# A hybrid decoder layer on one core: the first gate spread by POOL's queue one slab earlier, x's rows loaded slab by slab, the last modulation's bias from diagonal blocks

## The chip, the cores and the metric

The kernel runs on one core of a Trainium2 chip. The metric is the device time of one execution in microseconds; of several executions the median is given. Beside it stands one execution that the hardware profiler recorded, with a trace of every instruction.

## What is computed

One layer (DEPTH = 1) of a conditioned decoder trunk on x of 256 rows and 2048 columns, all in float32. The parts that matter here, cut from the reference:

```
mod = (c_act @ ada_w[l] + ada_b[l])[:, None, :]
sh1, sc1, g1, sh2, sc2, g2 = jnp.split(mod, N_MOD, axis=-1)
h = modulate(rms_norm(x, norm1_g[l]), sh1, sc1)
proj = h @ w_in[l] + b_in[l]
...
merged = gate_lru * (y_lru @ w_lru_out[l]) + gate_attn * (y_attn @ w_attn_out[l])
x = x + g1 * (merged @ w_o[l])
h2 = modulate(rms_norm(x, norm2_g[l]), sh2, sc2)
gate, up = jnp.split(h2 @ w_ffn_in[l], 2, axis=-1)
x = x + g2 * ((jax.nn.silu(gate) * up) @ w_ffn_out[l])
...
return rms_norm(x, final_g)
```

The six modulation vectors come from one vector c through a 2048 x 12288 matrix. g1 is the first gate, g2 the last modulation; final_g is the gain of the last norm.

## The kernel before, in words

**Items.** All large products are a list of items, made by `add_slab` and its relatives in the order in which they run: w_in, the gates of the recurrent branch, w_lru, the gates of the attention branch, w_att, w_o, the first and the second FFN matrix. An item is one weight load `raw` of 128 partitions x 1024 float32 (512 KB). Each weight is split into a high part `hi` (ACT, L305) and the rest `lo` (DVE, L317), and each product is three matmuls (hi with hi, hi with lo, lo with hi), L355 to L357. An item of w_att or w_o has twelve matmuls of 512 columns: two 128-row pieces of the weight, two halves of the 256 rows, three products. Eight items make a slab of 512 output columns; `wa` and `wo` are the sums in PSUM. In a slab's last item the matmuls of the first half of the rows stand first.

**Order.** Nothing is reordered by a scheduler: each engine and each queue runs in the order in which `step` writes the program. Per item, `step` issues the load six items ahead (L288), makes `hi` four ahead and `lo` three ahead, calls what is hung onto the item (`before`), writes the matmuls, and lets "sides" put in their own work while a clock of estimates says that there is room (`run_sides`, with an allowance `clock["slack"]`). What follows a slab is a generator in `posts`, one step of it per item. All loads and stores are DMAs on SP's queue; a DMA there waits until its buffer is free, and those behind it wait with it. Rows of POOL are few.

**Buffers.** `raw` has five buffers, `hi` four, `lo` three; everything of 4 KB per partition that lives longer (`b4`) shares 25.

**The modulation.** Five of the six vectors are sums over the columns of a transposed matrix: 158 loads `aw` of 512 KB, one DVE pass each (L496), with the row `crow` as the second operand; `modc[:, m, kt]` gets the results, the first gate (m = 2) ahead of the two parts of the second norm. The last one, g2, is needed as a row: `ada_rows` adds 32 loads `aw` of ada_g, scaled by c, into `pa` (L685, one DVE pass each, two per 128 rows), and a product with a matrix of ones (L691) sums the partitions. `pa` uses the buffer of `crow` and is set up like this:

```
        pa = ap_.tile([P, D], F32, tag="pal", name="pa")
        nc.gpsimd.memset(pa, 0.0)
        nc.sync.dma_start(pa[0:1, :], bg_row)
```

**The first gate and w_o.** g1 lies in 16 columns of `modc`. `gate_rows` transposes them on PE (L1011), copies the 16 x 128 result (ACT, L1013), writes it to DRAM as `g1d` (L1015) and reads it back twice, spread over all partitions (L1018). `load_rows` loads x's rows, four tiles `xr` of 512 columns (L1034). Both are hung onto the fourth item of w_o's first slab (`late` 6 means the weight's rows from 6 x 128 on). After each of the first three slabs `o_post` multiplies by the gate (L1055), adds x (L1057), takes squares and stores the rows as `x1d` (L1041).

**The second norm.** `second_norm` follows w_o's last slab: product with the gate and x's row (L1100, L1101), squares, root, transposes on PE (L1080), and the scaled, shifted rows for the first FFN slab `fg`. `ada_ffn`, the side that runs `ada_rows`, goes on before and after it.

**The last stage.** The second FFN matrix is done in two halves of the columns. Rounds of items alternate: two plain ones and four in which seven products stand for eight (L355 to L357 into `pp`, `pq`, `pr`, `pu`), whose third and fourth weights `made` are differences taken on DVE (L418 to L425, tile `last`). When the first half's last item is done, the post of `blocks(0, 2)` adds four blocks to x (L1415, L1417) and then multiplies by the final gain (L1441), once per half of the rows.

Of the kernel before, what the change touches and what calls it, by code (L numbers as in the profile page):

```python
# [11 lines left out]
AF = mybir.ActivationFunctionType  # L12
# [4 lines left out]
P = 128  # L17
D = 2048
S = 256
NK = D // P  # L20
# [13 lines left out]
V_ADA = V_CB + 64  # L34
# [23 lines left out]
SLACK = (2.0, 2.0)  # L58
# [14 lines left out]

@with_exitstack
def hybrid_layer(
    ctx: ExitStack, tc, vecs, x_t, x_r, ada_k, ada_t, ada_g, w_in, bv_row, bm_row, bg_row, lru_w, w_lru, w_att, w_o,
    w_f1, w_f2a, w_f2d, w_f2b, w_f2c, fg_row, out,
):
    nc = tc.nc
# [44 lines left out]
    vec = const.tile([P, NV], F32, name="vec")  # L124
# [18 lines left out]
    ident = const.tile([P, P], F32, name="ident")  # L143
# [134 lines left out]
    items = []  # L278
# [389 lines left out]
    def ada_rows():  # L668

        got = Halves([ada_g[kt, :, j * CH:(j + 1) * CH] for kt in range(NK) for j in range(2)])  # L670
        got.spare = lambda: len(got.got) - got.own < N_SPARE
        yield 0, 0, 0, 0, lambda: ada.cost is None
        streams.append(got)
        got.fetch()

        pa = ap_.tile([P, D], F32, tag="pal", name="pa")
        nc.gpsimd.memset(pa, 0.0)
        nc.sync.dma_start(pa[0:1, :], bg_row)
        for kt in range(NK):
            for j in range(2):  # L680
                if not got.got:
                    got.fetch()
                yield CH * T_DVE, 0, 0, 0, got.here
                p = pa[:, j * CH:(j + 1) * CH]
                nc.vector.scalar_tensor_tensor(p, got.take(), cact[:, kt:kt + 1], p, op0=ALU.mult, op1=ALU.add)  # L685
                got.fetch()
        for c in range(4):
            yield 0, 0, 0, 1
            pb = mtile(f"pb{c}")
            cs = slice(c * 512, (c + 1) * 512)  # L690
            nc.tensor.matmul(pb, lhsT=ones, rhs=pa[:, cs], start=True, stop=True)  # L691
            yield 0, 0.55
            nc.scalar.copy(pa[:, cs], pb)
            free(m=1)
        bcs[5] = pa
# [311 lines left out]
    def gate_rows():  # L1007
        while not {(2, kt) for kt in range(NK)} <= cols_done:
            ada.advance(True)
        ps = mtile("g1_ps")  # L1010
        nc.tensor.transpose(ps[0:NK, 0:P], modc[:, 2, :], ident)  # L1011
        row = sp.tile([P, S], F32, tag="t2", name="g1_row")
        nc.scalar.copy(row[0:NK, 0:P], ps[0:NK, 0:P])  # L1013
        free(m=1)
        nc.sync.dma_start(g1d, row[0:NK, 0:P])  # L1015
        for i in range(2):
            g1.append(b4(f"g1{i}", F32, (CH,)))
            nc.sync.dma_start(  # L1018
                g1[i], g1d[8 * i:8 * i + 8, :].rearrange("k p -> (k p)").partition_broadcast(P)
            )  # L1020

    for s in range(4):
        add_slab(w_att[s], f"wa{s}", aact, 0, NK, att_post(s), True)


    x1d = dp.tile([S, D], F32, name="x1d")
# [1 line left out]
    xr, x1T, pts = [], {}, {}  # L1028
    ss2 = const.tile([P, 2, 4], F32, name="ss2")

    def load_rows():
        for s in range(4):
            xr.append(b4(f"xr{s}", F32, (2, 512)))
            nc.sync.dma_start(xr[s], x_r[:, s * 512:(s + 1) * 512].rearrange("(t p) n -> p t n", p=P))  # L1034

    def w_o_first():
        load_rows()
        gate_rows()

    def keep_rows(s):  # L1040
        nc.sync.dma_start(x1d[:, s * 512:(s + 1) * 512].rearrange("(t p) n -> p t n", p=P), xr[s])  # L1041
# [23 lines left out]

    mact = of(m_hi, m_lo)

    def x_first():
        ada.finish(halves.fetch)

    for s in range(4):
        add_slab(w_o[s], f"wo{s}", mact, 0, NK, o_post(s), True, (w_o_first, None, None, x_first)[s], 6 if s == 0 else 0)

    def turn(p, of_w=False):

# [14 lines left out]

    def second_norm(banks):
        sides[:] = [ada_ffn]
        both = h2["both"] = hp.tile([P, NK, 2, S], F32R, tag="h", name="h2_both")
        hh, hl = both[:, :, 0, :], both[:, :, 1, :]

# [330 lines left out]
    def blocks(n0, n1):  # L1426

        def post():
            last = None
            for n in range(n0, n1):  # L1430
                for t in range(2):
                    g = residual(t, n)
                    next(g)
                    if last is not None:
                        next(last, None)
                    last = g
                    yield 1.2, 0.7
            next(last, None)
            for t in range(2):
                x2 = fin["x2"][:, t, n0 * 512:n1 * 512]  # L1440
                nc.vector.tensor_tensor(x2, x2, fin["fg"][:, n0 * 512:n1 * 512], op=ALU.mult)  # L1441
                yield 0.6 * (n1 - n0), 0.7 * (1 - t)
        return post
# [191 lines left out]
def _layout(i):  # L1635
# [6 lines left out]
    def slabs(w):  # L1642
        n = w.shape[1] // 512
        return w.reshape(NK, P, n, 512).transpose(2, 1, 0, 3).reshape(n, P, NK * 512)

    def pairs(w):
# [15 lines left out]
    made = {  # L1662
        "vecs": vecs, "x_t": f("x")[0].T.reshape(NK, P, S).transpose(1, 0, 2), "x_r": f("x")[0], "ada_k": a_k,
        "ada_t": a_t, "ada_g": ada_w[:, 5 * D:].reshape(NK, P, D),
        "w_in": slabs(f("w_in")[0]), "bv_row": f("b_in")[0, 6656:7168], "bm_row": f("b_in")[0, 7168:], "bg_row": ada_b[None, 5 * D:], "lru_w": lru,
        "w_lru": slabs(f("w_lru_out")[0]), "w_att": slabs(f("w_attn_out")[0]), "w_o": slabs(f("w_o")[0]),
        "w_f1": slabs(f("w_ffn_in")[0]), "w_f2a": w2[:, :CH].reshape(NH, P, CH),
        "w_f2d": w2[:EARLY * P, CH:].reshape(EARLY, P, CH),
# [23 lines left out]
```

## Time and profile before

| | |
|---|---|
| median of 3 runs | 1564.82 us (1564.37 to 1568.53) |
| profiled execution | 1562.41 us, of which the span of instructions 1560.6 us |
| TensorE (PE) busy | 1534.3 us, 98% |
| VectorE (DVE) busy | 1392.5 us, 89% |
| ScalarE (ACT) busy | 853.5 us, 55% |
| GpSimd (POOL) busy | 3.8 us |
| DMA | 400.38 MB, mean 257 GB/s |
| mean granted TensorE clock | 0.994 of full |

Times inside the profile are microseconds from the start of the span. "PE" is the matmuls, "SPq" the DMA queue of SP. A row of the timeline gives start, length, engine, line and operation, what is written <- what is read, the count, and in brackets how long the engine was idle just before and what ended that. A busy PE is a PE that has matmuls in its pipe; its clock is shown apart, in tenths or as a share of full speed.

### The profile page before, as it was taken

Reading aid. Unit: us, or ns where it says so; the run is one execution under the profiler, and the core shown is the slowest. Engines: PE = TensorE matmul, PEld = TensorE weight load, DVE = VectorE, ACT = ScalarE, POOL = GpSimd, SP = SyncE. Lnnn points to the kernel's source line nnn. Section 1 sums busy time; section 2 is a strip of 40 time slices with the busy share of each in tenths; the row PEclk is TensorE's granted clock in tenths of the full one; section 3 lists DMA queues with packets and bytes.
Section 4 is the critical chain, followed back from the end, with each engine's and each line's share of the span. In section 5 each row is a group of like instructions: output and inputs, shape, how many; then the busy total and the mean of one; then the engine's idle time right before and its main releaser. Section 6 shows DMA issues by size and latency. Waiting matters only on the chain.

```text
span 1560.6 us, 22091 instructions
## 1 busy us (share of the span) xinstructions
PE 1534.3 (98%) x8013; PEld 1316.3 (84%) x8013; DVE 1392.5 (89%) x1854; ACT 853.5 (55%) x1097; POOL 3.8 (0%) x9
## 2 busy tenths in 40 slices
PE   8999999999999999999899999999999999999997
PEld 7999999998878787888687788888888888888786
DVE  7889988999888888998689889999999999998998
ACT  4654443766855455444245655555555555664664
POOL 0000000000000000000000000000000000000000
PEclk9999999999999999999899999999999999999999
DMA  9999998665877897998999655665665656766563
GB/s 365 350 321 336 339 315 286 206 234 169 288 272 251 284 326 279 361 343 300 333 374 334 212 181 194 198 201 194 200 201 192 211 194 226 259 204 203 187 211 126
DMA packets 112911, 400.38 MB, mean 257 GB/s; under 512 B 12433, under 2 KB 12577, under 8 KB 112417
## 3 DMA queue, kind: packets, MB, share of 16 engines
q1 hardware_dynamic: 112514, 398.46, 74.2%
q8 instruction: 62, 1.02, 0.3%
q10 hardware_dynamic: 288, 0.52, 0.1%
q14 instruction: 47, 0.39, 0.1%
HBM read 394.73 MB, written 4.20 MB: 256 GB/s over the span
## 4 chain that ended last, share of the span: by engine, by line
PE 91%; DMA 5%; DVE 2%; issue 1%; SPq 0%; ACT 0%; DVEq 0%; ACTq 0%
PE pf L1345 9%; PE f L357 7%; PE f L356 7%; PE f L355 7%; PE wi L357 6%; PE wi L356 6%; PE wi L355 6%; PE wga L357 2%; PE wga L355 2%; PE wga L356 2%; PE wa L357 2%; PE wa L356 2%; PE wa L355 2%; PE wl L356 2%; PE wl L357 2%; PE wl L355 2%
## 5 line engine op out<-in xcount | busy, mean ns | idle before, releaser
L305 ACT CAST hi<-raw 128x1024 fp32r<-128x1024 f32 (+1 forms) x540 | 536.9, 1002 | 461.7 <-PE wi L356 82.0
L317 DVE TENSOR_TENSOR lo<-raw,hi 128x1024 fp32r<-128x1024 f32 (+1 forms) x540 | 618.9, 1160 | 66.8 <-issue 35.3
L357 PE MATMUL wi<-h_both,lo 128*128 128x256 f32 x800 | 227.3, 284 | 3.4 <-DVE lo L317 3.4
L355 PE MATMUL wi<-h_both,hi 128*128 128x256 f32 x800 | 228.0, 285 | 0.0
L356 PE MATMUL wi<-h_both,hi 128*128 128x256 f32 x800 | 227.0, 284 | 0.0
L355 PE MATMUL f<-hi,h_both 128*128 128x512 f32 x460 | 180.2, 392 | 0.0
L357 PE MATMUL f<-hi,h_both 128*128 128x512 f32 x460 | 179.0, 389 | 0.0
L356 PE MATMUL f<-lo,h_both 128*128 128x512 f32 x460 | 179.0, 389 | 0.0
L357 PEld LDWEIGHTS wi<-h_both,lo 128*128 128x128 f32 x800 | 154.2, 193 | 3.8 <-DVE lo L317 3.8
L355 PEld LDWEIGHTS wi<-h_both,hi 128*128 128x128 f32 x800 | 154.3, 193 | 0.2
L356 PEld LDWEIGHTS wi<-h_both,hi 128*128 128x128 f32 x800 | 154.2, 193 | 0.2
L305 ACT CAST hi<-made 128x1024 fp32r<-128x1024 f32 x60 | 63.4, 1056 | 112.8 <-PE f L357 111.0
L496 DVE CUSTOM_DVE_ANT_0 aw<-aw,crow,vec 128x1024 f32<-128x1024 f32 x79 | 100.7, 1279 | 5.6 <-DMA aw<-in_ada_t_dram 5.6
L496 DVE CUSTOM_DVE_ANT_0 aw<-aw,crow,modc 128x1024 f32<-128x1024 f32 x79 | 101.0, 1281 | 5.1 <-DMA aw<-in_ada_t_dram 5.0
L357 PEld LDWEIGHTS f<-hi,h_both 128*128 128x128 f32 x460 | 86.3, 188 | 17.9
L356 PEld LDWEIGHTS f<-lo,h_both 128*128 128x128 f32 x460 | 86.4, 188 | 17.8 <-issue 0.2
L355 PEld LDWEIGHTS f<-hi,h_both 128*128 128x128 f32 x460 | 86.4, 188 | 17.8 <-issue 0.2
L317 DVE TENSOR_TENSOR lo<-made,hi 128x1024 fp32r<-128x1024 f32 x60 | 73.4, 1225 | 25.7 <-PE f L356 20.4
L1345 PE MATMUL pf<-hi,fc 128*128 128x512 f32 x256 | 71.0, 389 | 0.0
L305 ACT CAST hi<-last 128x1024 fp32r<-128x1024 f32 x32 | 33.7, 1054 | 52.5 <-PE pf L1345 47.2
L685 DVE SCALAR_TENSOR_TENSOR pa<-aw,cact,pa 128x1024 f32<-128x1024 f32 x32 | 41.0, 1282 | 20.8 <-DMA aw<-in_ada_g_dram 20.2
L1345 PEld LDWEIGHTS pf<-hi,fc 128*128 128x128 f32 x256 | 48.1, 188 | 10.0
(353 smaller groups left out, 2954.4 us busy)
## 6 DMA issues: line engine op xcount, KB each, us to landing
raw<-in_w_f_dram SPq DMA_DIRECT2D x176, 512.0 KB, 3.9
raw<-in_w_in_dram SPq DMA_DIRECT2D x164, 512.0 KB, 6.7
aw<-in_ada_t_dram SPq DMA_DIRECT2D x158, 512.0 KB, 6.4
raw<-in_w_f2a_dram SPq DMA_DIRECT2D x44, 512.0 KB, 4.4
raw<-in_w_f2d_dram SPq DMA_DIRECT2D x36, 512.0 KB, 4.2
raw<-in_w_lru_dram SPq DMA_DIRECT2D x32, 512.0 KB, 6.5
raw<-in_w_att_dram SPq DMA_DIRECT2D x32, 512.0 KB, 8.1
raw<-in_w_o_dram SPq DMA_DIRECT2D x32, 512.0 KB, 7.7
```

Of the source, the lines that this page charges most:

```text
L305: nc.scalar.copy(hi[:, cs], live[i][0][:, cs])
L317: nc.vector.tensor_tensor(lo[:, cs], raw[:, cs], f32(hi[:, cs]), op=ALU.subtract)
L355: nc.tensor.matmul(ps, lhsT=lh, rhs=rh, start=start, stop=False, skip_group_check=True)
L356: nc.tensor.matmul(ps, lhsT=lh, rhs=rl, start=False, stop=False, skip_group_check=True)
L357: nc.tensor.matmul(ps, lhsT=ll, rhs=rh, start=False, stop=stop, skip_group_check=True)
L496: nc.vector.tensor_tensor_reduce(out=r, in0=r, in1=crow[:, j * CH:(j + 1) * CH], op0=ALU.mult, op1=ALU.add, scale=1.0, scalar=dst if j els ...
L685: nc.vector.scalar_tensor_tensor(p, got.take(), cact[:, kt:kt + 1], p, op0=ALU.mult, op1=ALU.add)
L1345: nc.tensor.matmul(bank(t, n), lhsT=l[:, rows(t)], rhs=w[:, c0:c0 + 512], start=kt == 0 and k == 0, stop=kt == (EARLY - 2 if (t, n) == (1, ...
```

## The change

`pa` gets its start from ACT: for each of the 16 column blocks of 128 the identity matrix, scaled per partition by the bias, so that the sum over partitions is the bias row; the memset, the bias row and its input go. `gate_rows` is hung onto the first item of the last w_att slab and its three DMAs are issued on POOL's queue. x's rows are loaded one slab at a time: the first at the second item of w_o's first slab, the others at the first item of theirs. From w_o's next to last item on no side gets room, until `second_norm` gives it back. In `blocks` the two multiplies by the final gain stand six steps later each, where two column blocks are done together.

```diff
@@ hybrid_layer
-    ctx: ExitStack, tc, vecs, x_t, x_r, ada_k, ada_t, ada_g, w_in, bv_row, bm_row, bg_row, lru_w, w_lru, w_att, w_o,
+    ctx: ExitStack, tc, vecs, x_t, x_r, ada_k, ada_t, ada_g, w_in, bv_row, bm_row, lru_w, w_lru, w_att, w_o,
@@ ada_rows
         pa = ap_.tile([P, D], F32, tag="pal", name="pa")
-        nc.gpsimd.memset(pa, 0.0)
-        nc.sync.dma_start(pa[0:1, :], bg_row)
+        for h in range(2):
+            yield 0, 1.9
+            for kt in range(h * NK // 2, (h + 1) * NK // 2):
+                v = V_ADA + 5 * NK + kt
+                nc.scalar.activation(pa[:, rows(kt)], ident, AF.Copy, scale=vec[:, v:v + 1])
@@ gate_rows
-        nc.sync.dma_start(g1d, row[0:NK, 0:P])
+        nc.gpsimd.dma_start(g1d, row[0:NK, 0:P])
         for i in range(2):
             g1.append(b4(f"g1{i}", F32, (CH,)))
-            nc.sync.dma_start(
+            nc.gpsimd.dma_start(
                 g1[i], g1d[8 * i:8 * i + 8, :].rearrange("k p -> (k p)").partition_broadcast(P)
             )
     for s in range(4):
-        add_slab(w_att[s], f"wa{s}", aact, 0, NK, att_post(s), True)
+        add_slab(w_att[s], f"wa{s}", aact, 0, NK, att_post(s), True, gate_rows if s == 3 else None)
...
-    def load_rows():
-        for s in range(4):
+    def load_rows(s):
+        def before():
             xr.append(b4(f"xr{s}", F32, (2, 512)))
             nc.sync.dma_start(xr[s], x_r[:, s * 512:(s + 1) * 512].rearrange("(t p) n -> p t n", p=P))
-
-    def w_o_first():
-        load_rows()
-        gate_rows()
+            if s == 3:
+                ada.finish(halves.fetch)
+        return before
...
-    def x_first():
-        ada.finish(halves.fetch)
-
     for s in range(4):
-        add_slab(w_o[s], f"wo{s}", mact, 0, NK, o_post(s), True, (w_o_first, None, None, x_first)[s], 6 if s == 0 else 0)
+        add_slab(w_o[s], f"wo{s}", mact, 0, NK, o_post(s), True, load_rows(s), 2 if s == 0 else 0)
+
+    def hold_sides():
+
+        clock["slack"] = -1e9
+        return 0, 0
+
+    items[-2].before.append(hold_sides)
@@ second_norm
         sides[:] = [ada_ffn]
+        clock["slack"] = SLACK[1]
@@ blocks, post
             for t in range(2):
+
+                for _ in range(6 * (n1 - n0 - 1)):
+                    yield 0, 0
                 x2 = fin["x2"][:, t, n0 * 512:n1 * 512]
                 nc.vector.tensor_tensor(x2, x2, fin["fg"][:, n0 * 512:n1 * 512], op=ALU.mult)
```

The order of the instructions at three places, before and in the changed kernel. Lines of the changed kernel are its own, a few higher than those of the profile; numbers in names tell buffers apart.

SP's queue in w_o's first slab before: x's rows, the write of the gate and its two spread reads stand between a load of ada_g and the next weight of w_o.

```order
L467 DMA aw_7440<-in_ada_g_dram 128x1024
L1034 DMA xr_7442<-in_x_r_dram 128x2x512
L1034 DMA xr_7444<-in_x_r_dram 128x2x512
L1034 DMA xr_7446<-in_x_r_dram 128x2x512
L1034 DMA xr_7448<-in_x_r_dram 128x2x512
L1015 DMA g1d<-g_row 16x128
L1018 DMA g_7455<-g1d 128x1024
L1018 DMA g_7457<-g1d 128x1024
L288 DMA raw_7475<-in_w_o_dram 128x1024
L467 DMA aw_7481<-in_ada_g_dram 128x1024
```

The same stretch of SP's queue now, from the second load of ada_g on.

```order
L467 DMA aw_7330<-in_ada_g_dram 128x1024
L288 DMA raw_7352<-in_w_o_dram 128x1024
L467 DMA aw_7358<-in_ada_g_dram 128x1024
L288 DMA raw_7382<-in_w_o_dram 128x1024
L467 DMA aw_7388<-in_ada_g_dram 128x1024
L288 DMA raw_7406<-in_w_o_dram 128x1024
L1037 DMA xr_7412<-in_x_r_dram 128x2x512
L288 DMA raw_7427<-in_w_o_dram 128x1024
L467 DMA aw_7433<-in_ada_g_dram 128x1024
L288 DMA raw_7458<-in_w_o_dram 128x1024
```

One load of x's rows is left here, between two weights; the three DMAs of the gate stand at the end of POOL's rows.

```order
L823 AFFINE_SELECT mask<-mask 128x128
L827 AFFINE_SELECT mask<-mask 128x128
L1018 DMA g1d<-g_row 16x128
L1021 DMA g_7185<-g1d 128x1024
L1021 DMA g_7187<-g1d 128x1024
```

DVE at the end of w_o before (`lo` are the subtracts, `pa` the passes of ada_g, `yo` the second norm's product with the gate).

```order
L317 TENSOR_TENSOR lo_8020<-raw_7954,hi_7997 128x1024
L685 SCALAR_TENSOR_TENSOR pa<-aw_7981,cact,pa 128x1024
L317 TENSOR_TENSOR lo_8041<-raw_7975,hi_8018 128x1024
L685 SCALAR_TENSOR_TENSOR pa<-aw_8001,cact,pa 128x1024
L317 TENSOR_TENSOR lo_8060<-raw_7995,hi_8039 128x1024
L685 SCALAR_TENSOR_TENSOR pa<-aw_8022,cact,pa 128x1024
L1100 TENSOR_TENSOR yo_8098<-wo_0_0_7916,g_7457 128x512
L1101 TENSOR_TENSOR xr_7448<-xr_7448,yo_8098 128x512
```

And now.

```order
L317 TENSOR_TENSOR lo_8034<-raw_7968,hi_8011 128x1024
L688 SCALAR_TENSOR_TENSOR pa<-aw_7995,cact,pa 128x1024
L317 TENSOR_TENSOR lo_8055<-raw_7989,hi_8032 128x1024
L317 TENSOR_TENSOR lo_8073<-raw_8009,hi_8053 128x1024
L1107 TENSOR_TENSOR yo_8110<-wo_0_0_7930,g_7187 128x512
L1108 TENSOR_TENSOR xr_7928<-xr_7928,yo_8110 128x512
```

Two passes of `pa` are gone from here; they stand in the second FFN slab `fu`, behind its last subtracts.

DVE in the last stage before, in the round that follows the first half's last item (`last` is the tile of made weights and of the rows with the final gain).

```order
L425 TENSOR_TENSOR last<-raw_13124,last 128x512
L317 TENSOR_TENSOR lo_13202<-raw_13124,hi_13174 128x1024
L1441 TENSOR_TENSOR last<-last 128x1024
L317 TENSOR_TENSOR lo_13222<-last,hi_13200 128x1024
L1441 TENSOR_TENSOR last<-last 128x1024
L317 TENSOR_TENSOR lo_13233<-last,hi_13220 128x1024
```

Now the first multiply stands a round later, ahead of both subtracts of made weights, and the second one two rounds later, between them.

```order
L317 TENSOR_TENSOR lo_13306<-raw_13253,hi_13282 128x1024
L1451 TENSOR_TENSOR last<-last 128x1024
L317 TENSOR_TENSOR lo_13325<-last,hi_13304 128x1024
L317 TENSOR_TENSOR lo_13334<-last,hi_13323 128x1024
L317 TENSOR_TENSOR lo_13346<-raw_13300,hi_13332 128x1024
...
L317 TENSOR_TENSOR lo_13410<-last,hi_13390 128x1024
L1451 TENSOR_TENSOR last<-last 128x1024
L317 TENSOR_TENSOR lo_13420<-last,hi_13408 128x1024
```

Each multiply is thus apart from the other, with at least a whole round of items between them. On ACT, which has no place of its own here, the 16 blocks of `pa` stand as two runs of eight behind the last casts of w_att, with one cast between them.

## Rows read from the trace of the kernel before

**Rows 1.** Page, part 1: busy time, share of the span and instructions

```profile
PE 1534.3 (98%) x8013; PEld 1316.3 (84%) x8013; DVE 1392.5 (89%) x1854; ACT 853.5 (55%) x1097; POOL 3.8 (0%) x9
```

**Rows 2.** PE's waits: waiting and releasing lines, us in total, times, longest

```profile
PE wo L355 <- ACT hi L305: 4.9, 1, 4.9
...
PE wo L356 <- DVE lo L317: 2.6, 1, 2.6
...
PE r_ps L1119 <- ACT yo L1116: 0.9, 1, 0.9
PE pt L1080 <- DVE xr L1101: 0.8, 1, 0.8
PE pq L356 <- DVE lo L317: 0.6, 1, 0.6
PE pr L356 <- DVE lo L317: 0.6, 1, 0.6
```

**Rows 3.** PE's timeline, 762 to 784 us

```profile
761.78 0.39 PE L356 MATMUL wo<-lo,mh 128*128 128x512 f32 x1
...
767.45 0.39 PE L357 MATMUL wo<-hi,ml 128*128 128x512 f32 x1
772.78 0.80 PE L355 MATMUL wo<-hi,mh 128*128 128x512 f32 x1 [4.94 <-ACT hi L305]
...
782.31 0.39 PE L356 MATMUL wo<-lo,mh 128*128 128x512 f32 x1
```

**Rows 4.** Windows: stretch, length, each engine's busy us (count), granted clock, DMA share, GB/s

```profile
700.00:730.00 30.00, 30.00 (x142) 24.99 (x142) 27.41 (x34) 13.34 (x15) 0.00 (x0) 1.00 0.98 338
768.00:778.00 10.00, 2.60 (x5) 1.78 (x6) 4.11 (x4) 2.49 (x3) 0.00 (x0) 0.68 1.01 374
800.00:820.00 20.00, 20.00 (x90) 16.56 (x89) 17.26 (x15) 9.87 (x12) 0.00 (x0) 1.00 1.02 382
```

**Rows 5.** Waits of SP's queue, 735 to 860 us

```profile
SPq L678 <- POOL pa L677: 8.6, 1, 8.6
SPq L1018 <- DMA g1d<-g_row: 7.6, 1, 7.6
```

**Rows 6.** Timeline of SP's queue, 740 to 870 us: when DMAs are issued

```profile
756.63 0.48 SPq L1015 DMA_DIRECT2D g1d<-g_row  x1
...
765.72 0.42 SPq L288 DMA_DIRECT2D raw<-in_w_o_dram  x1
```

**Rows 7.** DVE's timeline, 736 to 738 us: the last pass with crow

```profile
737.21 0.08 DVE L496 DVE_READ_ACCUMULATOR2_ANT modc<- 128x1 f32 x1
```

**Rows 8.** ACT's timeline in the second norm

```profile
846.38 0.40 ACT L1116 ACTIVATE yo<-ident,sr 128x128 f32<-128x128 f32 x1 [0.23 <-DVE sr L1111]
```

**Rows 9.** ACT's timeline, 700 to 742 us: casts of the last w_att slab

```profile
734.22 1.05 ACT L305 CAST hi<-raw 128x1024 fp32r<-128x1024 f32 x1 [1.66 <-PE wa L357]
```

**Rows 10.** PE's timeline at w_o's end

```profile
841.04 0.39 PE L357 MATMUL wo<-hi,ml 128*128 128x512 f32 x1
```

**Rows 11.** DVE's timeline there

```profile
840.92 1.28 DVE L685 SCALAR_TENSOR_TENSOR pa<-aw,cact,pa 128x1024 f32<-128x1024 f32 x1
842.12 0.68 DVE L1100 TENSOR_TENSOR yo<-wo,g 128x512 f32<-128x512 f32 x1
```

**Rows 12.** DVE's timeline in the last stage, first round of the second half

```profile
1446.88 1.22 DVE L1441 TENSOR_TENSOR last<-last 128x1024 f32<-128x1024 f32 x1
```

**Rows 13.** DVE's timeline, an undisturbed round of the last stage

```profile
1478.59 1.22 DVE L317 TENSOR_TENSOR lo<-last,hi 128x1024 fp32r<-128x1024 f32 x1
1480.07 1.23 DVE L317 TENSOR_TENSOR lo<-last,hi 128x1024 fp32r<-128x1024 f32 x1 [0.27 <-ACT hi L305]
```

**Rows 14.** PE's timeline in the same round

```profile
1481.01 0.39 PE L356 MATMUL pr<-lo,ah 128*128 128x512 f32 x1
...
1482.37 0.39 PE L356 MATMUL pq<-lo,ah 128*128 128x512 f32 x1
```

**Rows 15.** DVE's timeline: first product with the gate

```profile
777.51 0.69 DVE L1055 TENSOR_TENSOR yo<-wo,g 128x512 f32<-128x512 f32 x1
```

More of the change, by code (lines that the diff above doesn't have):

```diff
@@ L1664, in _layout @@
         "ada_t": a_t, "ada_g": ada_w[:, 5 * D:].reshape(NK, P, D),
-        "w_in": slabs(f("w_in")[0]), "bv_row": f("b_in")[0, 6656:7168], "bm_row": f("b_in")[0, 7168:], "bg_row": ada_b[None, 5 * D:], "lru_w": lru,
+        "w_in": slabs(f("w_in")[0]), "bv_row": f("b_in")[0, 6656:7168], "bm_row": f("b_in")[0, 7168:], "lru_w": lru,
         "w_lru": slabs(f("w_lru_out")[0]), "w_att": slabs(f("w_attn_out")[0]), "w_o": slabs(f("w_o")[0]),
```

## The prediction

> **What bounds the kernel now.** I read the page first: TensorE is busy 98% of the span [rows 1]. So only time in which PE waits, or runs slowly, can be given back, and the second view, PE's waits, says where: among others 4.9 and 2.6 us in the matmuls of w_o, 0.9 and 0.8 us in the second norm, twice 0.6 us in the last stage [rows 2]. At these three places the diff changes something. PE's timeline shows the first one in full [rows 3]. From 761.78 to 767.45 us 26 matmuls start, 25 steps of 0.2268 us. Then PE stands still until 772.78 and, after one matmul, once more, and the 16th matmul after the one at 772.78 starts at 782.31. Undisturbed it would have started at 767.45 + 17 x 0.2268 = 771.31. The place costs 11.0 us: 7.56 us of waits, and 3.4 us because the granted clock, 1.00 in the stretches before and behind, is 0.68 here [rows 4], a step towards the lower of its two levels (1.2 and 2.4 GHz) after the idle time.
>
> What made PE wait is read off SP, whose queue issues every load in the program's order. Its own waits show two long ones that are no waits for a used buffer: 8.6 us for POOL (the bias row waits for the memset of pa) and 7.6 us for the write of g1d [rows 5]. The write is issued at 756.63 and the next weight load, behind it in the queue, at 765.72 [rows 6]: no load leaves for 9 us, and PE runs dry two us later. The first hole, before 739, led to no wait of PE; the lead in the buffers covered it.
>
> **The change part by part.**
>
> *Gate to POOL's queue, one slab earlier.* One transpose, one copy on ACT and three DMAs leave the place between the x rows and the weights. On SP nothing waits for a DRAM write any more. On PE the transpose stands ahead of the last attention slab: its input, the modulation's gate part, is the first of three parts of a stream whose last pass ends at 737.3 [rows 7], so it is long there; on ACT the copy stands between casts; on POOL nothing is behind the DMAs. The two spread loads are 1 MB: at 338 GB/s, the rate around that slab [rows 4], 3.1 us of transfers, most of which falls where SP now waits anyway (below). Gain: the whole place, 11.0 us. The bounds: 7.6 us if a slow clock still came from elsewhere, 11.0 if nothing takes the wait's place. I take 11.0, since with no wait of PE there is nothing ahead of a fall of the clock.
>
> *Bias from diagonal blocks.* Memset, bias row and SP's wait for them go. Sixteen ACT instructions of 128x128 come, two runs of eight with a cast between. The nearest row is the same form in the second norm, 0.40 us [rows 8]: at most 3.2 us a run. They need the buffer of crow, free at 737.3 [rows 7]. ACT has 1.66 us idle ahead of each cast [rows 9], one cast per item of 2.72 us (12 x 0.2268). So the runs push the next two casts by 1.5 and 3.1 us; a cast is made four items, 10.9 us, ahead of its matmuls. Cost 0; without that lead it would be 6.4 us. SP still stops there: the second ada_g load needs a buffer which the pass ending at 737.3 frees. The hole loses only what followed that pass, the memset, and it cost PE nothing before. Gain 0.
>
> *x's rows slab by slab.* Four 512 KB loads that stood together now stand one per slab; three move into the w_o stage. From the second ada_g load to the last w_o weight the new order has 57 loads of 524,288 bytes, 29.9 MB. They may start at 737.3 and must be there about when PE comes to the last w_o item: its twelve matmuls end with the one at 841.04 [rows 10], so it begins at 838.5, without the 11 us at 827.5, less 2.3 us for cast and subtract, so 88 us. At 382 GB/s, which this stage moved without a wait of PE, they take 78 us; at 338 GB/s, in the attention branch, 88.5 [rows 4]. I take 0, the stage's own rate being the nearer row, and keep up to 4.1 us: three loads of 1.37 us (524,288 bytes at 382 GB/s), each in front of a weight at the head of a slab.
>
> *Sides held in the last two w_o items.* Two passes of pa, 1.28 us each, leave DVE's queue ahead of the second norm. Now the last one starts at 840.92 and the norm's first instruction directly behind it at 842.12 [rows 11]. Its input, the first half of the last item (sorted first), has its last matmul six steps before the one at 841.04, at 839.7, so it may start near 840.4; the second half's end near 841.5 then sets the pace: 1.3 to 1.8 us earlier. PE's waits there are 0.8 + 0.9 = 1.7 us [rows 2], which is the most that can come back; bounds 0 and 1.7, I take 1.5. The passes come back in the second FFN slab's stretch, 2.6 us of DVE where it has waits of its own; the matmuls that need them are put one item later. Cost 0, and 1.3 us if a matmul there meets the last pass.
>
> *The two multiplies by the final gain.* Each is 1.22 us on DVE [rows 12] and stands right in front of a subtract that PE waits for 0.6 us: 1.2 us in all. They move one and two rounds of 10.2 us later. What they meet there is read in an undisturbed round: the two subtracts start at 1478.59 and 1480.07 (after an idle 0.27) and take 1.2 us [rows 13]; PE uses them at 1481.01 and 1482.37 [rows 14], so 1.2 and 1.1 us are to spare. Starts of such instructions are 1.13 apart. The first multiply takes 1.13 of 1.2: no wait. After the idle 0.27 a lag of 0.86 remains; the second adds 1.13, less 0.27: 1.72 against 1.1, so PE waits 0.6 there. Net gain 0.6, bounds 0 and 1.2.
>
> **Sum.** 11.0 + 1.5 + 0.6 = 13.1 us. The profiled execution took 1562.4 (span 1560.6 and 1.8 around it), so it would be 1549.3. The runs' median is 1564.8, 2.4 above it; measured times are compared with that: 1564.8 - 13.1 = 1551.7 us.
>
> **The rivals.**
>
> *Transfers give part of it back.* The weights come late at the heads of slabs, or the stage becomes bound by DMA. For it: the windows show a DMA share of 1.00 and more all through w_o [rows 4], and SP stops for each store of a slab as before. Against it: the stage now starts with full buffers, not after a hole, and PE never waited at this load after 782. Price 2 to 4.1 us, so 1553.7 to 1555.8. Everything is lost only below 29.9 MB / (88 + 11) us = 302 GB/s.
>
> *The gate comes too late.* This is the one that ends slower. The gate's rows are first used by the product at 777.51 [rows 15], 766.5 without the stall; it stands in DVE's queue with every later subtract behind it, and PE has at most two items, 5.4 us, in hand. If POOL's loads land after 772, PE waits for them, and from about 785 on (13.1 us more) the change is a loss; landing at 790 would give 1551.7 + 18 = 1569.7. They leave some 22 us (one slab of eight items) before w_o starts at 742, so they have over 50 us for what took SP 9 us [rows 6]. By the rows that is out of reach. The Trainium skill, page "SBUF — State Buffer", section "SBUF: two separate sides", has the rule that speaks against the move: descriptors of a DMA from POOL's queue are written by GpSimd, which some VectorE instructions lock out. No run here shows a DMA from that queue; DVE is idle 2.6 of 30 us there [rows 4], and a lock would have to hold through all of that. By that rule alone the time would be over 1564.8.
>
> *The stall stays.* The first hole, hardly shorter, is what starves w_o, and the second only the last drop. For it: SP still waits to 737.3. Against it: PE's waits name no other place before 767 in this stage [rows 2]. It would give back half of the 11.0 or more: 1557 to 1563.
>
> **How the numbers follow.** The forecast, with 1549.5 to 1553.5 as its own range, 0.72; transfers 0.17; the stall stays 0.08; the gate late 0.03. The range of 8 in 10 takes the forecast and most of the transfers: 1549.0 to 1557.0. A difference under 0.3%, 4.7 us, can't be told from none here. Faster by more (under 1560.1) are the forecast, the transfers and a part of the third: 0.92; the same 0.05; slower 0.03.
>
> **What would show it.** Right: no wait of SP for POOL or g1d; no wait of PE and clock 1.00 from 742 to w_o's end, with w_o's matmuls over in 88 us; the norm's product without a pa pass ahead of it and PE's waits there under 0.4; no wait at the old place of the gain's multiply, at most one of 0.6 some 20 us on. Wrong: PE waits for a w_o weight behind a load of x; ACT's casts late behind the sixteen blocks; DVE waiting for the gate's rows.

## The result, and the profile after

The changed kernel takes 1551.49 us (median of 4 runs, 1549.47 to 1554.48), beside 1564.59 us for the kernel before (4 runs, 1562.26 to 1568.53): a ratio of 0.9915, 95% interval 0.9889 to 0.9942, so 13.1 us less. The forecast was 1551.7. The profiled execution has a span of 1547.7 us, 12.9 less than that of before.

Page of the changed kernel, part 1 (answers to [rows 1]), and the lines on this place from its list of PE's waits (answers to [rows 2]).

```profile
PE 1530.9 (99%) x8013; PEld 1314.2 (85%) x8013; DVE 1392.2 (90%) x1854; ACT 858.2 (55%) x1113; POOL 3.7 (0%) x11
```

```profile
PE r_ps L1126 <- ACT yo L1123: 0.8, 1, 0.8
...
PE pq L356 <- DVE lo L317: 0.2, 1, 0.2
PE pr L356 <- DVE lo L317: 0.2, 1, 0.2
```

No wait in w_o is left. Windows in the columns of [rows 4], the first over the last attention slab, the others over w_o: PE never runs out, at a clock of 1.00, also where it stood before.

```profile
700.00:730.00 30.00, 30.00 (x142) 24.94 (x141) 27.29 (x34) 13.43 (x16) 1.70 (x3) 1.00 0.98 339
...
742.00:762.00 20.00, 20.00 (x94) 16.62 (x94) 18.88 (x19) 10.97 (x18) 0.00 (x0) 1.00 1.00 377
768.00:778.00 10.00, 10.00 (x46) 8.29 (x45) 8.41 (x8) 4.40 (x7) 0.00 (x0) 1.00 1.03 362
820.00:830.00 10.00, 10.00 (x46) 8.27 (x45) 7.00 (x7) 3.31 (x4) 0.00 (x0) 1.00 1.01 352
```

PE's timeline of the changed kernel: w_o's first and last matmul, the second norm's product of ones, and the first of fg.

```profile
742.51 0.39 PE L355 MATMUL wo<-hi,mh 128*128 128x512 f32 x1
...
830.21 0.39 PE L357 MATMUL wo<-hi,ml 128*128 128x512 f32 x1
...
834.95 0.70 PE L1126 MATMUL r_ps<-yo,ones 128*128 128x256 f32 x2 [0.84 <-ACT yo L1123]
...
836.82 0.50 PE L355 MATMUL fg<-hi,h_both 128*128 128x512 f32 x1
```

From the first matmul of w_o to the start of its last one took 87.70 us; before it was 98.86 (742.18 to 841.04). From there to fg's first matmul it is 6.61, before 7.66, by this row of PE's timeline of before:

```profile
848.70 0.50 PE L355 MATMUL fg<-hi,h_both 128*128 128x512 f32 x1
```

From the first `pp` of the last stage to the last it is 0.7 less (1320.0 to 1506.9 against 1331.9 to 1519.5). So the trace's ledger reads 11.2 + 1.05 + 0.7 = 12.9, with w_o beginning 0.3 later and 0.3 less at the end.

The gate's DMAs on POOL's queue (timeline, then DMA issues with KB and median us to landing).

```profile
721.40 0.63 POOL L1018 DMA_DIRECT2D g1d<-g_row  x1 [495.82 <-ACT g_row L1016]
727.32 1.07 POOL L1021 DMA_DIRECT2D g<-g1d  x2 [5.29 <-DMA g1d<-g_row]
```

```profile
g<-g1d POOLq DMA_DIRECT2D x2, 512.0 KB, 8.6
...
g1d<-g_row POOLq DMA_DIRECT2D x1, 8.0 KB, 5.4
```

The slower of the two reads landed 10.0 us after its issue at 727.9, by 738. The first product with the gate starts at 764.84, so there were 27 us to spare.

SP's timeline: the loads of ada_g on either side of the one hole that is left, and the w_o weight that now stands between them. ACT's timeline: the two runs of blocks, with the cast between.

```profile
730.49 0.33 SPq L467 DMA_DIRECT2D aw<-in_ada_g_dram  x1
732.91 0.33 SPq L288 DMA_DIRECT2D raw<-in_w_o_dram  x1
737.65 0.33 SPq L467 DMA_DIRECT2D aw<-in_ada_g_dram  x1
```

```profile
739.09 2.45 ACT L681 ACTIVATE pa<-ident,vec 128x128 f32<-128x128 f32 x8
741.45 1.03 ACT L305 CAST hi<-raw 128x1024 fp32r<-128x1024 f32 x1
742.38 2.45 ACT L681 ACTIVATE pa<-ident,vec 128x128 f32<-128x128 f32 x8
```

DVE's timeline at w_o's end (answers to [rows 11]): the norm's product starts 0.03 us after w_o's last matmul starts, where it was 1.08. The pass ahead of it waited 1.39 us for its load of ada_g, and two subtracts stand between.

```profile
826.71 1.28 DVE L688 SCALAR_TENSOR_TENSOR pa<-aw,cact,pa 128x1024 f32<-128x1024 f32 x1 [1.39 <-DMA aw<-in_ada_g_dram]
827.91 2.41 DVE L317 TENSOR_TENSOR lo<-raw,hi 128x1024 fp32r<-128x1024 f32 x2
830.24 0.68 DVE L1107 TENSOR_TENSOR yo<-wo,g 128x512 f32<-128x512 f32 x1
```

PE's timeline in the last stage: what is left of the two waits of 0.61 and 0.62, at the multiplies' new places, 12 us apart.

```profile
1447.19 0.50 PE L356 MATMUL pr<-lo,ah 128*128 128x512 f32 x1 [0.22 <-DVE lo L317]
...
1459.28 0.50 PE L356 MATMUL pq<-lo,ah 128*128 128x512 f32 x1 [0.24 <-DVE lo L317]
```

### The profile page after: what moved, and what is told of

The parts are those of the page before. It is cut to its first block, busy times and chain, and to the rows that moved or that the text cites. A ratio compares the mean times of both kernels' runs of the same rounds, so it can differ in the third digit from the quotient of the medians.

```text
span 1547.7 us, 22116 instructions
## 1 busy us (share of the span) xinstructions
PE 1530.9 (99%) x8013; PEld 1314.2 (85%) x8013; DVE 1392.2 (90%) x1854; ACT 858.2 (55%) x1113; POOL 3.7 (0%) x11
## 4 chain that ended last, share of the span: by engine, by line
PE 93%; DMA 4%; DVE 2%; issue 1%; ACT 0%; SPq 0%; DVEq 0%; ACTq 0%
PE pf L1352 9%; PE f L356 7%; PE f L357 7%; PE f L355 7%; PE wi L357 6%; PE wi L355 6%; PE wi L356 6%; PE wga L357 2%; PE wga L355 2%; PE wga L356 2%; PE wa L357 2%; PE wa L355 2%; PE wa L356 2%; PE wl L356 2%; PE wl L357 2%; PE wl L355 2%
## 5 line engine op out<-in xcount | busy, mean ns | idle before, releaser
L355 PE MATMUL wl<-hi,yh 128*128 128x512 f32 x128 | 52.5, 410 | 0.0
```

Of the source, the lines that this page charges most:

```text
L355: nc.tensor.matmul(ps, lhsT=lh, rhs=rh, start=start, stop=False, skip_group_check=True)
```

## The experiments

The main theory: PE stalled in w_o because SP's queue stood for the write of g1d, and this alone was worth 11 us. The rivals: the place decides and not the queue; the holes and the loads add up, so that the stall only moves; the small edits carry more than their terms. Each kernel was timed against the kernel before. "w_o" is the time between the starts of its first and last matmul in the trace, "norm" that from there to fg's first matmul. All results stand in one table.

| kernel | median us | ratio (95% interval) | w_o | product after last matmul | norm |
|---|---|---|---|---|---|
| before | 1564.59 to 1565.87 | | 98.86 | +1.08 | 7.66 |
| changed | 1551.49 | 0.9915 (0.9889 to 0.9942) | 87.70 | +0.03 | 6.61 |
| gate_early_pool | 1558.76 | 0.9953 (0.9936 to 0.9971) | 90.30 | +3.62 | 11.32 |
| gate_early_sp | 1563.88 | 0.9992 (0.9979 to 1.0006) | 95.05 | +4.25 | 11.95 |
| gate_late_pool | 1561.83 | 0.9974 (0.9962 to 0.9987) | 94.17 | +4.82 | 12.53 |
| hold_alone | 1561.21 | 0.9972 (0.9958 to 0.9986) | 96.96 | -0.16 | 6.42 |
| two_edits | 1555.18 | 0.9941 (0.9924 to 0.9958) | 90.69 | -0.30 | 6.29 |
| three_edits | 1552.23 | 0.9922 (0.9900 to 0.9943) | 89.13 | +1.35 | 7.93 |
| x_together | 1551.05 | 0.9908 (0.9890 to 0.9926) | 89.47 | -0.13 | 6.44 |
| bias_row | 1551.02 | 0.9920 (0.9907 to 0.9934) | 87.71 | +0.86 | 7.45 |
| sides_free | 1555.54 | 0.9947 (0.9931 to 0.9964) | 88.33 | +4.68 | 12.39 |
| gain_old | 1553.35 | 0.9930 (0.9915 to 0.9946) | 87.71 | +1.03 | 8.53 |
| hold_earlier | 1553.40 | 0.9935 (0.9922 to 0.9948) | 88.29 | +1.72 | 8.30 |
| norm_first | 1550.17 | 0.9901 (0.9878 to 0.9924) | 87.71 | -0.93 | 5.70 |

The kernel before was timed again beside each group of kernels, and its five medians run from 1564.59 to 1565.87; a difference between two rows of the table carries that much besides the spread of the runs. How finely a trace can be read is in the table too: the changed kernel and gain_old are the same program up to the last stage, and their norms differ by 1.9 us; bias_row and three_edits are the same up to there, and w_o differs by 1.4. A trace is one execution: that of gate_early_pool took as long as the kernel's median, those of gate_early_sp, gate_late_pool and sides_free 3.4, 2.8 and 4.1 us longer.

The last column holds two things. Where the norm's product starts less than 2 us after w_o's last matmul, fg's first matmul follows the product by 6.6 us, in all traces but gain_old's. In the four kernels where it starts 3.6 to 4.8 us after, PE waits in the norm for 3.1 to 4.1 us until the rows can be transposed, the granted clock falls to 0.50, the lower of its two levels, and fg follows the product by 7.7 us. In gain_old's trace, at +1.03, it fell as well (7.5 us); in those of before, three_edits and hold_earlier, at +1.08 to +1.72, it did not. These 0.9 to 1.1 us are a second price of a late product. PE's timeline and windows before fg in gate_early_pool, then the window of the changed kernel:

```profile
838.91 0.33 PE L1079 MATMUL pt<-ident,xr 128*128 128x128 f32 x1 [2.07 <-DVE xr L1100]
...
842.15 1.22 PE L1118 MATMUL r_ps<-yo,ones 128*128 128x256 f32 x2 [0.92 <-ACT yo L1115]
```

```profile
842.15:845.15 3.00, 3.00 (x12) 2.82 (x13) 1.50 (x4) 1.16 (x3) 0.00 (x0) 0.50 0.98 271
```

```profile
833.82:836.82 3.00, 2.10 (x15) 1.67 (x13) 1.45 (x6) 1.25 (x4) 0.00 (x0) 1.00 1.01 335
```

**The gate alone, on POOL's queue.** On the kernel before, the two reads of g1d likewise, and `gate_rows()` out of `w_o_first`:

```diff
-        nc.sync.dma_start(g1d, row[0:NK, 0:P])
+        nc.gpsimd.dma_start(g1d, row[0:NK, 0:P])
-        add_slab(w_att[s], f"wa{s}", aact, 0, NK, att_post(s), True)
+        add_slab(w_att[s], f"wa{s}", aact, 0, NK, att_post(s), True, gate_rows if s == 3 else None)
```

> The kernel before with the first edit alone: the gate's rows at the first item of the last w_att slab, their three DMAs on POOL's queue. x's four loads, the bias row, the sides and the final gain stay as before. Theory: the write of g1d in SP's queue is the whole cause of PE's stall in w_o, so all of the 11.0 us comes back: about 1553.6 us, no wait of PE in w_o, granted clock 1.00 from 742 on. Rival, the holes add up: the wait for the memset to 739 and x's four loads in a row (four times 1.37 us) still starve w_o; PE waits 1.4 to 4.1 us there and the clock falls again: 1555 to 1560 us.

Measured 7.1 us less (4.5 to 10.0 by the interval), inside the rival's range: PE waits 2.0 us in w_o, though its clock stays at 1.00 there. w_o is 8.6 us shorter than in the trace of before, and then the norm is 3.7 longer, 1.1 of it the clock. The timelines of DVE and PE show both remainders: in w_o a pass waits for a load of ada_g that stands behind x's four loads, the next subtract stands behind the pass, and PE waits for it (1.22 and then 0.74 us); at the end other passes wait, and the norm's product stands behind them, 3.62 us after the last matmul at 833.83.

```profile
768.04 1.28 DVE L685 SCALAR_TENSOR_TENSOR pa<-aw,cact,pa 128x1024 f32<-128x1024 f32 x1 [5.58 <-DMA aw<-in_ada_g_dram]
...
770.51 0.50 PE L356 MATMUL wo<-lo,mh 128*128 128x512 f32 x1 [1.22 <-DVE lo L317]
...
836.24 1.28 DVE L685 SCALAR_TENSOR_TENSOR pa<-aw,cact,pa 128x1024 f32<-128x1024 f32 x1 [1.40 <-DMA aw<-in_ada_g_dram]
837.45 0.68 DVE L1099 TENSOR_TENSOR yo<-wo,g 128x512 f32<-128x512 f32 x1
```

**The place without the queue.** As above, but with `nc.sync` for all three DMAs.

> The same early place, but the three DMAs stay on SP's queue. If the place decides: 1553.6 us as with POOL's queue, since SP's hole of about 7.6 us falls where the loads run six items ahead. If the queue decides: SP stands for the write near 721 us, where the DMA share is 0.98, the loads behind it come up to 7.6 us late, and PE waits 2 to 8 us in the last w_att slab or at the head of w_o: 1556 to 1562 us.

2.0 us less, within its interval of no change (-0.9 to 3.3), and 1.9 us above the range that the queue's theory gave. So the early place by itself is worth little. Timelines of SP and of DVE:

```profile
724.09 0.34 SPq L1015 DMA_DIRECT2D g1d<-g_row  x1
728.04 0.81 SPq L1018 DMA_DIRECT2D g<-g1d  x2
...
745.72 0.28 SPq L678 DMA_DIRECT2D pa<-in_bg_row_dram  x1
```

```profile
736.28 1.29 DVE L496 CUSTOM_DVE_ANT_0 aw<-aw,crow,vec 128x1024 f32<-128x1024 f32 x1 [4.07 <-DMA aw<-in_ada_t_dram]
```

SP stands 3.5 us for the write, half of what it did in w_o, in a stretch whose DMA share is 0.97 with the same DMAs on POOL's queue (700 to 730) and 0.86 here. The modulation's passes then come late (4.07 us of waiting), and the hole that waits for the last of them ends at 745.7 where it ended at 739.2. Of these 6.5 us 3.1 lie ahead of the attention branch (wa begins at 655.6, before at 652.5), so against that branch it ends 3.4 us later. w_o still has waits of 1.3 and 2.1 us; it is 3.8 us shorter than before, and the norm is 4.3 longer. The write is not gone from the queue's sum, it has moved.

**The queue without the place.** On the kernel before, `nc.gpsimd` for the three DMAs where they stood.

> The old place (fourth item of w_o's first slab), but the three DMAs on POOL's queue. If the queue decides: SP no longer stands, and the gate lands about 757 + 5.4 + 7.2 to 10.0 = 770 to 773 us, where the first product wants it at 766.5; PE has two items, 5.4 us, in hand, so it waits 0 to 1 us: 1553.6 to 1555 us, with DVE waiting 3 to 6 us for the gate's rows. If being late counts in full: 1557 to 1560 us. If the place decides: 1564.6 us.

4.0 us less (2.0 to 6.0), between the ranges that were expected, and for another reason than a late gate. The gate's reads had landed by 773.6 (764.0 + 9.6), and DVE came to the product at 775.43 without a wait for them. It had waited 6.67 us for a load of ada_g, issued behind x's four loads:

```profile
770.08 1.28 DVE L685 SCALAR_TENSOR_TENSOR pa<-aw,cact,pa 128x1024 f32<-128x1024 f32 x1 [6.67 <-DMA aw<-in_ada_g_dram]
...
772.55 0.57 PE L356 MATMUL wo<-lo,mh 128*128 128x512 f32 x1 [2.41 <-DVE lo L317]
```

With the gate early on the same queue that wait was 5.58 us and PE's longest 1.22; here PE's is 2.41. The place alone gives 2.0 us, which is not clear of no change, the queue alone 4.0, both together 7.1: about the sum of the two, and for the whole both are needed. That the gate's 1 MB in flight beside x's rows makes the difference of place is argued, not shown.

**The changed kernel without the held sides** (`items[-2].before.append(hold_sides)` taken out).

> The changed kernel without holding the sides at w_o's end. By the prediction's term two passes of 1.28 us come back ahead of the norm's product: 1.0 to 1.5 us lost, about 1552.5 to 1553 us, the product 1.1 us after w_o's last matmul starts, as before. Rival, from the run with the gate alone: now that w_o runs without a stall, the loads of ada_g come late at its end, and the passes wait for them with the norm behind: the product starts 2 to 4 us after the last matmul, 3 to 4.6 us lost, 1554.5 to 1556 us.

The time is the rival's, 4.05 us over the changed kernel by the medians, and 5.8 us of norm in the trace, which is the slowest of the six executions. w_o has no wait of PE here. The passes come back; of the last four the first three wait for their loads, and the product stands behind the last, 4.68 us after the last matmul at 834.30. Of the 5.8 us 4.65 are the product's later start and 1.1 the clock, 0.90 in the mean of that stretch. DVE's timeline and the window:

```profile
829.43 1.28 DVE L688 SCALAR_TENSOR_TENSOR pa<-aw,cact,pa 128x1024 f32<-128x1024 f32 x1 [2.01 <-DMA aw<-in_ada_g_dram]
...
832.66 1.29 DVE L688 SCALAR_TENSOR_TENSOR pa<-aw,cact,pa 128x1024 f32<-128x1024 f32 x1 [0.80 <-DMA aw<-in_ada_g_dram]
...
835.23 1.28 DVE L688 SCALAR_TENSOR_TENSOR pa<-aw,cact,pa 128x1024 f32<-128x1024 f32 x1 [0.15 <-DMA aw<-in_ada_g_dram]
...
837.78 1.28 DVE L688 SCALAR_TENSOR_TENSOR pa<-aw,cact,pa 128x1024 f32<-128x1024 f32 x1
838.98 0.68 DVE L1106 TENSOR_TENSOR yo<-wo,g 128x512 f32<-128x512 f32 x1
```

```profile
820.00:846.00 26.00, 21.76 (x104) 17.66 (x103) 19.89 (x23) 10.31 (x19) 0.00 (x0) 0.90 0.88 316
```

**The held sides on the kernel before.**

> The kernel before with the sides held at w_o's end alone. By the prediction's term 1.5 us (measured in the changed kernel: the product 1.05 us earlier): about 1563.5 us. Theory that this edit's worth depends on the gate: here no more than these 1.0 to 1.5 us, against 4 us when it is left out of the changed kernel, because the stall in w_o gives the loads of ada_g time to catch up. Rival: 4 us here too, 1561 us.

3.9 us less by the runs (2.2 to 6.6), 1.2 by the norms of the two traces. The runs speak for the rival, that the edit's worth does not hang on the gate: 3.9 us where the stall is there, 4.05 where it is gone. So they speak against the theory that the stall gave the loads of ada_g time to catch up. The traces do not bear it out either. The last four passes ahead of the norm's product wait 1.7 us in sum for their loads in the trace of before, and 3.0 to 3.9 in the four other traces with free sides, whether PE had waited in w_o for 3.4 us (gate_early_sp), 3.3 (gate_late_pool), 2.0 (gate_early_pool) or not at all (sides_free). A likely reason is that the profile of before, 2.4 us below its median, caught an execution in which the last passes were early. That is not shown: there is one trace of before.

**The gate and the held sides together.**

> The kernel before with two of the edits alone: the gate early on POOL's queue, and the sides held at w_o's end. My theory now: with the gate alone the passes of ada_g come late at w_o's end (the product started 3.6 us after the last matmul), so the two edits together give what the gate alone did not, and the others next to nothing: about 1552 us, 0.8 us over the changed kernel for the final gain, fg beginning 6.6 us after w_o's last matmul. Rival: the bias blocks and the loads slab by slab are needed as well, w_o keeps the 2.0 us of waits that it had with the gate alone and the norm starts late: 1554 to 1556 us.

The norm is short (6.29), as the theory had it, but w_o keeps 2.1 us of waits and 90.7 us. The time is the rival's. The two edits give 9.9 us of the 13.1 (interval 6.6 to 11.9). Against hold_alone, timed beside it, the gate's edit gives 6.0 us here, and w_o falls by 6.3 (96.96 to 90.69): about what it gives without the held sides, not 11.

**And x's rows slab by slab with them.**

> The kernel before with three of the edits: the gate early on POOL's queue, the sides held, and x's rows slab by slab; the bias row and the place of the final gain as before. With the first two alone w_o took 90.3 us with 2.1 us of waits. If x's four loads in a row are what is left there: w_o in 87.7 us without a wait, and about 1552.3 us, 0.8 us over the changed kernel for the final gain. Rival: SP's wait for the memset is what is left, w_o stays at 89 to 90 us, 1554 to 1555 us.

The time is the theory's. The w_o of 90.3 us in the expectation is that of the gate alone; two_edits has 90.7. The trace is between: w_o at 89.13 with one wait of 1.0 us, where the same program with the final gain at its new place (bias_row) had 87.71 and none. x's rows are the likelier remainder: by the medians they give 3.0 us here, by intervals that overlap. The traces say which waits go: the two of 1.4 and 0.7 us in two_edits, at 769 and 773, behind a pass that waits 5.5 us for a load issued after x's four, have no counterpart here; the wait of 1.0 is at 807.

**x's rows together in the changed kernel**, at the second item of w_o's first slab.

```diff
-            xr.append(b4(f"xr{s}", F32, (2, 512)))
...
+            for q in range(4) if s == 0 else ():
+                xr.append(b4(f"xr{q}", F32, (2, 512)))
...
```

> The changed kernel with x's four loads together again, at the second item of w_o's first slab. My theory puts the loads slab by slab at no gain and no cost: the weights behind the four loads come 4.1 us later, which the lead covers, so 1551.5 us and no wait of PE in w_o. Rival, the spreading is a part of the gain: PE waits 1.4 to 4.1 us behind the four loads, near 755 to 765 us: 1553 to 1556 us or more if the clock falls with it.

No loss in time, and one wait of 0.5 us in w_o, at 796. In the changed kernel spreading the loads is worth nothing that the runs can tell. The four loads stand together here, two items earlier than before, and though a pass still waits 3.0 us behind them, PE does not: as far as one trace shows, it is their old place, at the fourth item, that made PE wait, and not their number.

**The memset and the bias row in the changed kernel.**

> The changed kernel with the memset and the bias row in SP's queue again. By the prediction's term 0: 1551.5 us, w_o's matmuls in 87.7 us, since the lead covers SP's wait. Rival, from the run with the gate alone: the weight that was issued at 732.9 between the two loads of ada_g stands behind the bias row until 739, some 6 us in which nothing is loaded, ahead of a stage that is near the limit of the transfers: PE waits 1 to 3 us in w_o, 1552.5 to 1555 us.

The prediction's term of 0 holds: w_o 87.71 without a wait, SP's 8.6 us for POOL covered by the lead.

**The multiplies at their old place in the changed kernel.**

> The changed kernel with the two multiplies by the final gain at their old place. Two waits of PE of 0.6 us each there in place of the two of 0.2 us that are left: 0.8 us lost, about 1552.3 us. The rival, that they cost nothing because DVE is behind either way, would show the same sum of waits. The time alone can hardly tell 0.8 us; the waits in the trace do.

PE's waits are 0.6 and 0.6 again. That is 0.8 us; the other 1.1 of the 1.9 us in the medians are within the interval. The norm of this trace was a slow one: the product 1.0 us later, and 0.9 more with the clock, which is 0.50 from 837 to 839.

**Sides held from one item earlier.**

> The changed kernel with the sides held from one item earlier on. In the changed kernel the norm's product starts at 830.24, directly behind two subtracts that a pass of ada_g held up, which itself waited 1.39 us for its load; the product's input is there at about 829.5. If that pass is what holds the product: it starts 0.5 to 0.7 us earlier against w_o's last matmul, 0.5 to 0.7 us gained, about 1551 us. Rival: the second half of the rows, whose last matmul ends near 830.6, sets the pace, so under 0.3 us, or the pass costs as much where it comes back.

It failed twice over. ACT's timeline: the cast of an FFN weight waits for its load. DVE's: with the pass gone the last subtract waits for that cast, and the product for the subtract. And PE's waits show the pass where it comes back, in front of the product that sums `pa`.

```profile
829.43 1.05 ACT L305 CAST hi<-raw 128x1024 fp32r<-128x1024 f32 x1 [1.53 <-DMA raw<-in_w_f_dram]
```

```profile
830.51 1.22 DVE L317 TENSOR_TENSOR lo<-raw,hi 128x1024 fp32r<-128x1024 f32 x1 [1.35 <-ACT hi L305]
831.65 0.68 DVE L1107 TENSOR_TENSOR yo<-wo,g 128x512 f32<-128x512 f32 x1
```

```profile
PE pb L694 <- DVE pa L688: 2.1, 1, 2.1
```

**The norm's product ahead of an FFN subtract, the final gain in four parts.** On the changed kernel, where `clock["norm"]` is w_o's last item; the multiplies are four of 512 columns, six steps apart:

```diff
+        late = i == clock.get("norm")
-        upto("hi", do_hi, i + N_HI)
-        upto("lo", do_lo, i + N_LO)
+        upto("hi", do_hi, i + N_HI - late)
+        upto("lo", do_lo, i + N_LO - late)
```

> The changed kernel with two more edits. At w_o's last item one cast and one subtract of an FFN weight are left for the next step, so that the norm's product is not behind them; and the multiplies by the final gain are four of 512 columns, six steps apart. If the subtract is what holds the product: it starts 0.7 to 1.0 us earlier against w_o's last matmul, fg about 1.0 us earlier; the two waits of 0.2 us in the last stage go: about 1550.2 us, which the time can hardly tell from the changed kernel and the trace can. Rival: the subtract and cast come in the way of the norm's later blocks, PE waits in fg and nothing is gained.

The product starts 0.96 us earlier against the last matmul, and fg 0.91; both waits of the last stage are gone. PE's timeline shows that fg gives it back, at a matmul behind the subtract that was put off:

```profile
840.09 0.50 PE L357 MATMUL fg<-lo,h_both 128*128 128x512 f32 x1 [0.95 <-DVE lo L317]
```

At 1550.17 us it is the lowest median of all, but its interval covers the changed kernel's.

## Why the prediction was right, step by step

- **Gate to POOL's queue: 11.0 forecast. All of it came back, but not by this edit alone.** In the changed kernel SP has no wait for POOL or g1d, w_o runs in 87.7 us where 88 was said, 11.2 less, and the clock stays at 1.00. The edit alone gives 7.1 us, and 6.0 beside the held sides. The step that failed is that nothing takes the wait's place: x's four loads at their old place do. PE waits 2.0 to 2.1 us behind them in gate_early_pool and two_edits; not a weight came late, as the rival on transfers has it, but a load of ada_g, whose pass holds up a subtract in DVE's order. "PE never waited at this load after 782" was read behind that place. In gate_early_pool the norm is 3.7 us longer as well; how much of that is the edit, and how much an early norm in the one trace of before, is open.
- **Sides held: 1.5 forecast, 1.05 in the trace against before; 3.9 by the runs alone, 4.0 when taken out.** The bound "the most that can come back", 1.7, was read from PE's waits in one execution of before, in which the last pass did not wait and the three ahead of it waited 0.54, 0.92 and 0.24 us. The two passes were counted by their length, 1.28 us each; they also cost their loads' lateness, and 1.1 us of clock in the traces where PE stands 3 us and more behind them. The product did not start ahead of the last matmul either: two subtracts stand in front of it. PE's wait of 0.8 for `r_ps` did not go under 0.4 for that reason: it follows the product's start, 0.84 us at +0.03, 0.65 at -0.16 (hold_alone), 0.51 at -0.30 (two_edits), none at -0.93 (norm_first).
- **Bias from diagonal blocks: 0, and 0.** The runs take 2.45 us each, under the 3.2 of the bound, SP still stops to 737.65, and no wait of PE follows.
- **x's rows slab by slab: 0 forecast, up to 3 in the experiments.** The term was mis-sized: with the four together at the fourth item a pass waits 5.5 to 6.7 us behind them as soon as the write no longer follows them in SP's queue, and PE about 2 us and more. Spreading them is worth 0 (x_together is 0.4 us under the changed kernel); taking them from that place is worth 3.0 by the medians of two_edits and three_edits, which the intervals do not separate from nothing.
- **The final gain: 0.6 forecast, 0.7 measured.** One new wait of 0.6 was expected at the second multiply and none at the first; it is 0.22 and 0.24, so the first place had some 0.2 us less room than was read, and the second 0.4 more.
- **The late gate**, the rival that ends slower, is refuted with 27 us to spare. The Trainium skill, page "SBUF — State Buffer", section "SBUF: two separate sides", has GpSimd kept from writing its descriptors by some VectorE instructions. Here the write landed in 5.4 us beside a DVE that was busy 27.3 of 30 us (gate_early_sp, on SP's queue: 3.9), and the reads in 7.2 and 10.0 (SP: 4.1 and 4.9). Slower by up to a factor of two, and with 27 us to spare no lock that mattered; which of DVE's instructions here are of the page's kind no run shows.

The sum was right because the stall and its price were read rightly and the edits together removed all of it. As worths of single edits three terms were off: the gate's by 4 to 5 us too high, the sides' by 2.4 too low, that of x's rows by up to 3 too low. That these cancel is luck.

## What to carry to other kernels

A write that is waited for can hold up every load behind it in its queue. SP's wait of 7.6 us for g1d went with 11.0 us lost on PE before, and its wait of 3.5 us at the early place with 5.1 us (1563.88 against 1558.76); but its wait of 8.6 us for POOL cost nothing in bias_row, where the lead in the buffers covered it. So such a write belongs in a queue with nothing behind it, and away from other bursts of loads. The Trainium skill, page "DMA: Bandwidth & Descriptors", section "Rules for kernel authors", says that spreading DMAs over queues does not help bandwidth and only saves issue time; here the same three DMAs at the same place differ by those 5.1 us, far more than the issue time of about 0.5 us each. And work whose loads may come late should not stand ahead of the next step on the path: two passes of 1.28 us there cost about 4 us, with the stall and without it.

## What was not expected of the hardware

The spread between executions of one program shows in the loads, and behind them in the clock. The kernel before ranged from 1559.1 to 1571.1 us in 22 runs, and two traces of one program (changed and gain_old) had the second norm at 6.6 and 8.5 us with the same instructions in the same order. One part is the loads of the last two passes: the last one started 3.5 us ahead of w_o's last matmul in the changed kernel (826.71 against 830.21) and 2.5 in gain_old (828.05 against 830.55). The other part, 0.9 us, is the clock: in gain_old the granted clock fell to 0.50 after PE's waits of 0.70 and 0.92 us in the norm, and in the changed kernel, after one of 0.84, it stayed at 1.00. In the trace of before waits of 0.75 and 0.92 left it at 1.00 too, so what made it fall is open. PE's row in gain_old, beside the 0.70 us for the same two matmuls above:

```profile
836.28 1.01 PE L1126 MATMUL r_ps<-yo,ones 128*128 128x256 f32 x2 [0.92 <-ACT yo L1123]
```

Bounds that are read from one trace of such a stage carry this spread.
